# A hybrid decoder block on one Trainium2 core: the projections of attention heads 0 to 3 in three panels of 512 features instead of six of 256

## The chip, the core and the metric

The kernel runs on one core of a Trainium2 chip. The metric is the device time of one execution in microseconds (us). Before the change the median of 3 runs was 982.01 us (981.92 to 983.61). TensorE is called PE here, VectorE DVE, ScalarE ACT, GpSimd POOL; SP is the engine whose queue issues most of the loads.

## What is computed

The block takes x (512 tokens by 1024 features, float32), normalises it to u, and projects u by one combined weight. Branch A is a gated delta rule (GDN) over chunks of 64 tokens, branch B is causal softmax attention with a forgetting bias (FOX), both of 8 heads of 128. The two are merged by gates, and an MLP follows. Cut from the reference:

```python
u = rmsnorm(x, norm_mix_g[l])
proj = u @ w_in[l]
(gq, gk, gv, gz, ga, gb, fq, fk, fv, ff, gate_a, gate_b) = jnp.split(proj, split_idx, axis=-1)
...
o_a = gated_delta_rule_chunked(qh, kh, vh, g, beta).transpose(0, 2, 1, 3)
...
fqh = rmsnorm(to_heads(fq, FOX_HEADS), fox_q_norm_g[l]).astype(f32)
fkh = rmsnorm(to_heads(fk, FOX_HEADS), fox_k_norm_g[l]).astype(f32)
fvh = to_heads(fv, FOX_HEADS).astype(f32)
log_f = jax.nn.log_sigmoid(ff.astype(f32) + fox_f_bias[l].astype(f32)).transpose(0, 2, 1)
o_b = forgetting_attention(fqh, fkh, fvh, log_f).transpose(0, 2, 1, 3)
...
merged = jax.nn.sigmoid(gate_a) * y_a + jax.nn.sigmoid(gate_b) * y_b
h = x + merged @ w_out[l]

hn = rmsnorm(h, norm_mlp_g[l])
x = h + jnp.square(jax.nn.relu(hn @ w_up[l])) @ w_down[l]
```

The change concerns `fq`, `fk` and `fv` of FOX heads 0 to 3: 4 heads x 3 x 128 = 1536 of the projected features, each a sum over 1024.

## The kernel before

**Split products.** A float32 operand is held as two parts, `hi` (rounded to the type that PE multiplies fast) and `lo` (the rest). Each product is made as hi·hi, hi·lo and lo·hi into the same PSUM bank.

**Units of weights.** Weights come in units of 128 x 1024 elements (512 KB). `load` (L200) puts a unit into one of three `raw` buffers by a DMA on SP's queue; `prefetch_split` (L243) casts it to `hi` on ACT (L256) and subtracts to `lo` on DVE (L257), into a pool `whl` that has four hi's and four lo's; `unit` (L260) hands out the next unit and keeps the splits two units ahead and the loads three ahead. A `raw` buffer is free once its `lo` is made, and a `hi` or `lo` once its last product is.

**PSUM.** `mmps` (L92) deals out three banks of 128 x 512 for the projections, in turn. Before a bank is filled again, what was in it must have been copied out.

**The stages** in the order of the program: the start and the first z gates (to 42 us); GDN group 0 (four heads); `fox_pair(0)` and `fox_pair(1)` (L950, about 122 to 213 us); three more z gates and GDN group 1 (to 325 us); a stream of projections for FOX heads 4 to 7 and the gates (L1011, to 535 us); the merge (to 620 us); the MLP (L1171, to 980 us).

**fox_pair** makes, for two heads, three panels of 256 features: q and k of the one head, q and k of the other, v of both. A panel takes two units, `us`, each with four of the eight slices of u's features. For each pair of token blocks (`t2`) one bank is taken; its left half is the first token block and its right half the second. Each token block gets 8 products hi·uhi (L961), 8 of hi·ulo (L962) and 8 of lo·uhi (L964), each 128 x 128 times 128 x 256. Then the bank is copied to the page `fqk`, whole on ACT (L969) for q and k, or half on ACT and half on DVE (L972) for v.

**Beside it** run generators: `tick()` (L127), which fox_pair calls after each token block's first block and after each bank (24 times in the two calls), lets each go on to its next `yield`. Those that matter here are, in this stretch,

- `head` and `invert` (L659) of GDN group 0: `kk` (L639) gives AT (L641), ACT lays out `dg` (L666), DVE transposes it to E (L669) and makes 31 x 2 steps of forward substitution in X (L681, L683), then Xd (L689) and XT (L692). ACT copies Xd into X2 (L698, L699) and XT into AT (L712). PE makes Qp (L707) from Xd, Tp and Tq (L720, L722) from a copy of it (L710), and then Q6 (L741) and T6 (L739);
- `fox_worker` (L866): the head's fq and fk are normalised (fss, L884 and L885), transposed (L898, L899), and its scores, softmax, and output follow (L919 to L947);
- `factors_u` (L426): loads four pages `ux` from DRAM (L432, SP's queue), scales them (L436, ACT), adds and subtracts (L448, DVE) and splits them (L286, L287). It is started between the two calls of fox_pair.

A list scheduler then orders each engine's instructions, ahead of time; on the chip every engine works its list in that order, and an instruction that waits holds up all behind it.

## Time and profile before

| what | value |
| --- | --- |
| median of 3 runs | 982.01 us (981.92 to 983.61) |
| span of the profiled execution, first to last instruction | 980.2 us |
| PE busy | 970.8 us, 99% |
| DVE, ACT, POOL busy | 710.9 (73%), 605.0 (62%), 240.2 us (25%) |
| granted PE clock | full in every slice of the span |
| DMA | 174.38 MB, mean 178 GB/s |

The profiled execution's own time is its span and what lies around it; only the span is shown. In the profile a line such as "124.44 0.96 PE fx L964 x8" in the chain is a start, a length and a count of instructions, and "fqk<-fx 128x512" in the timeline is an output, an input and the shape of one instruction; what stands in brackets is the time that the engine stood idle before, and whose end it had waited for. "L961 PE MATMUL ... x192 | 48.5, 288" is a group, its busy time in us and the mean ns of one; for PE these overlap, so that the steps from start to start are read from the chain.

### The profile page before, as it was taken

What the parts mean: (1) busy time and instruction counts of PE and PEld (TensorE: products, weight loads), DVE (VectorE), ACT (ScalarE), POOL (GpSimd) and SP (SyncE); (2) the same over time, 40 slices, a digit from 0 to 9 for tenths busy, and PEclk for the clock granted to TensorE, in tenths of its full rate; (3) what the DMA queues carried; (4) which work ended last, traced back from release to release, by engine and by line L of the source; (5) the groups of instructions that cost most, each with busy time, mean ns of one, the idle gap of its engine ahead of it and who ended that gap; (6) DMA issues with size and microseconds to landing.
All of it is one profiled execution on the core that took longest, in us unless ns stands there. A gap on an engine that the chain in (4) does not pass through costs nothing.

```text
span 980.2 us, 17198 instructions
## 1 busy us (share of the span) xinstructions
PE 970.8 (99%) x6545; PEld 874.8 (89%) x6545; DVE 710.9 (73%) x1204; ACT 605.0 (62%) x1050; POOL 240.2 (25%) x236
## 2 busy tenths in 40 slices
PE   8999999999999999999999999999999999999998
PEld 6788899998888999999999888889989989988986
DVE  6877778566577789855656535889896697698596
ACT  7766444766564787867656422678755765666761
POOL 1544120202533513522320005312121121121110
PEclk9999999999999999999999999999999999999999
DMA  7647662475437885757887735688798888889884
GB/s 266 213 135 223 174 158 90 130 239 181 129 116 228 189 166 141 197 129 166 236 201 215 273 103 171 125 181 173 190 188 196 187 173 206 181 175 202 186 166 119
DMA packets 93442, 174.38 MB, mean 178 GB/s; under 512 B 8016, under 2 KB 49200, under 8 KB 93360
## 3 DMA queue, kind: packets, MB, share of 16 engines
q1 hardware_dynamic: 78928, 120.85, 38.8%
q0 software_dynamic: 14432, 52.44, 30.5%
q8 instruction: 51, 0.84, 0.4%
q14 instruction: 31, 0.25, 0.1%
HBM read 152.25 MB, written 21.02 MB: 177 GB/s over the span
## 4 chain that ended last, share of the span: by engine, by line
PE 92%; DVE 4%; DMA 2%; ACT 1%; issue 1%; SPq 0%; DVEq 0%
PE mlp L1171 36%; PE st L1011 12%; PE mm L279 8%; PE mm L276 8%; PE mm L275 8%; PE fx L964 2%; PE fx L961 2%; PE fx L962 2%; PE fo L944 2%; PE sc L919 1%; PE pT L935 1%; DVE lo L257 1%; PE kk L639 1%; PE kq L647 1%; DMA ux<-ud 1%; PE v L797 1%
## 5 line engine op out<-in xcount | busy, mean ns | idle before, releaser
L1402 ACT CAST hi<-draw 128x1024 fp32r<-128x1024 f32 x124 | 130.0, 1050 | 118.4 <-PE mlp L1171 100.4
L1409 DVE TENSOR_TENSOR lo<-draw,hi 128x1024 fp32r<-128x1024 f32 x124 | 151.3, 1222 | 44.8 <-ACT hi L1402 41.6
L256 ACT CAST hi<-raw 128x1024 fp32r<-128x1024 f32 (+1 forms) x62 | 62.9, 1021 | 82.6 <-PE mm L276 59.5
L1171 PE MATMUL mlp<-hi,shi 128*128 128x512 f32 x280 | 109.5, 391 | 0.1
L1171 PE MATMUL mlp<-hi,slo 128*128 128x512 f32 x280 | 109.1, 390 | 0.0
L1171 PE MATMUL mlp<-lo,shi 128*128 128x512 f32 x280 | 109.0, 389 | 0.0
L257 DVE TENSOR_TENSOR lo<-raw,hi 128x1024 fp32r<-128x1024 f32 (+1 forms) x62 | 73.9, 1197 | 29.1 <-ACT hi L256 13.4
L1171 PE MATMUL mlp<-shi,lo 128*128 128x256 f32 x448 | 90.3, 283 | 0.0
L1171 PE MATMUL mlp<-slo,hi 128*128 128x256 f32 x448 | 90.3, 283 | 0.0
L1171 PE MATMUL mlp<-shi,hi 128*128 128x256 f32 x448 | 90.3, 283 | 0.0
L276 PE MATMUL mm<-ulo,hi 128*128 128x512 f32 x216 | 85.0, 394 | 1.2 <-DVE ulo L290 1.2
L275 PE MATMUL mm<-uhi,hi 128*128 128x512 f32 x216 | 85.0, 395 | 0.0
L257 DVE TENSOR_TENSOR lo<-sraw,hi 128x1024 fp32r<-128x1024 f32 x49 | 60.7, 1240 | 20.9 <-ACT hi L256 20.1
L1171 PEld LDWEIGHTS mlp<-shi,hi 128*128 128x128 f32 x448 | 70.6, 192 | 0.9
L1171 PEld LDWEIGHTS mlp<-shi,lo 128*128 128x128 f32 x448 | 69.9, 192 | 0.0
L1171 PEld LDWEIGHTS mlp<-slo,hi 128*128 128x128 f32 x448 | 69.8, 192 | 0.0
L256 ACT CAST hi<-sraw 128x1024 fp32r<-128x1024 f32 x49 | 51.3, 1047 | 26.6 <-PE st L1011 16.2
L1171 PEld LDWEIGHTS mlp<-hi,shi 128*128 128x128 f32 x280 | 52.6, 188 | 11.1 <-issue 0.7
L1171 PEld LDWEIGHTS mlp<-lo,shi 128*128 128x128 f32 x280 | 52.6, 188 | 11.1
L1171 PEld LDWEIGHTS mlp<-hi,slo 128*128 128x128 f32 x280 | 52.6, 188 | 10.3
L219 POOL DMA_DIRECT2D draw<-w_d x30 | 26.3, 876 | 129.9 <-DVE lo L1409 120.8
L219 POOL DMA_DIRECT2D draw<-w_u x32 | 27.7, 866 | 122.6 <-DVE lo L1409 120.0
(336 smaller groups left out, 2466.6 us busy)
## 6 DMA issues: line engine op xcount, KB each, us to landing
draw<-w_u POOLq DMA_DIRECT2D x32, 512.0 KB, 5.7
draw<-w_d POOLq DMA_DIRECT2D x32, 512.0 KB, 6.5
sraw<-w_st POOLq DMA_DIRECT2D x28, 512.0 KB, 5.9
draw<-w_d SPq DMA_DIRECT2D x26, 512.0 KB, 4.4
raw<-w_gdn SPq DMA_DIRECT2D x24, 512.0 KB, 3.8
draw<-w_u SPq DMA_DIRECT2D x24, 512.0 KB, 4.4
sraw<-w_st SPq DMA_DIRECT2D x21, 512.0 KB, 5.5
hd<-hd SPq DMA_DIRECT2D x34, 256.0 KB, 5.4
```

What stands on the lines that cost most here:

```text
L219: nc.gpsimd.dma_start(raw, a[w][c, q, s_], accum_op=ALU.add)
L256: act.copy(hi[:, c], raw[:, c])
L257: vec.tensor_tensor(lo[:, c], raw[:, c], hi[:, c].bitcast(F32), op=ALU.subtract)
L275: mm(o, w, rhi(k), start=(k == 0), stop=False)
L276: mm(o, w, rlo(k), start=False, stop=False)
L279: mm(o, lo[:, k * cols:(k + 1) * cols], rhi(k), start=False, stop=(k == KT - 1))
L944: mm(po[:, cs(i)], vt[c], st[i][:, cs(c)], start=(c == 0), stop=(c == i))
L961: mm(o, uhi[k][:, cs(tb)], w, start=(k == 0), stop=False)
L1011: mm(o, u, w, start=first and t == 0 and k == 0 and j == 0 and x is hi, stop=x is lo and k == 3, skip_group_check=True)
L1171: return (lambda *args, **kw: tc.keep_in_program_order(f(*args, **kw))) if self.pinned[0] else f
L1402: pact.copy(hi, raws[m][0])
L1409: pvec.tensor_tensor(lo, raws[m][0], hi[:, :].bitcast(F32), op=ALU.subtract)
```

## The change

fox_pair, called twice with three panels of 256 features, becomes `fox_panel`, called three times with a panel of 512 features: q and k of heads 0 and 1, v of heads 0 to 3, q and k of heads 2 and 3. A panel takes four units, each with two of the eight slices of u's features. It makes two passes (`half`) over them; in a pass two banks are open, each for one token block and all 512 features, and a unit's products go to both. In the first pass the units are taken one after the other, and they are held for the second: `held` stops prefetch_split at the panel's four units, and in the second pass it is raised by one after each unit, with the split and the load called from there. After each unit comes a `tick()`: 8 in a panel, 24 in all. A bank is copied out on ACT alone, as two copies of 128 x 256 (one for each head) or one of 128 x 512 (v). v of all four heads is there after the second panel; factors_u starts after the first. The weights' layout in DRAM follows the panels.

```diff
+    held = [None]
+
     def prefetch_split(n):
-        while len(units) < min(len(seq), n):
+        while len(units) < min(len(seq), n, len(seq) if held[0] is None else held[0]):
...
-    def fox_pair(hp):
-        vts = ([], [])
-        for pn in range(3):
-            us = [unit("w_fox"), unit("w_fox")]
-            pg2 = [page(s="fqk"), page(s="fqk")]
-            for t2 in range(2):
-                ps = mmps("fx")
-                for tb in (2 * t2, 2 * t2 + 1):
-                    o = ps[:, (tb % 2) * 256:(tb % 2 + 1) * 256]
...
+    def fox_panel(heads):
+
+        n0 = pos[0]
+        held[0] = n0 + 4
+        us = []
+        pgs = {h: [page(s="fqk"), page(s="fqk")] for h in heads}
+        vp = []
+        for half in range(2):
+            ps = {tb: mmps("fx") for tb in (2 * half, 2 * half + 1)}
+            for j in range(4):
+                if not half:
+                    us.append(unit("w_fox"))
+                hi, lo = us[j]
+                for tb, o in ps.items():
+                    for k in (2 * j, 2 * j + 1):
+                        w = hi[:, (k % 2) * T:(k % 2 + 1) * T]
                         mm(o, uhi[k][:, cs(tb)], w, start=(k == 0), stop=False)
                         mm(o, ulo[k][:, cs(tb)], w, start=False, stop=False)
+                for tb, o in ps.items():
+                    for k in (2 * j, 2 * j + 1):
+                        mm(o, uhi[k][:, cs(tb)], lo[:, (k % 2) * T:(k % 2 + 1) * T], start=False, stop=(k == KT - 1))
+                if half:
+                    held[0] = n0 + 5 + j if j < 3 else None
+                    prefetch_split(n0 + 5 + j)
+                    prefetch_raw(n0 + 6 + j)
+                tick()
+            for tb, o in ps.items():
+                if heads:
+                    for i, h in enumerate(heads):
+                        act.copy(pgs[h][half][:, (tb % 2) * 256:(tb % 2 + 1) * 256], o[:, i * 256:(i + 1) * 256])
                 else:
+                    v = page(s="fqk")
+                    act.copy(v, o)
+                    vp.append(v)
+        for h in range(G):
+            vts[h].extend(v[:, cs(h)] for v in vp)
+        for h in heads:
+            fq.append((h, pgs[h], vts[h]))
...
-    fox_pair(0)
+    fox_panel((0, 1))
     fu = start(factors_u())
-    fox_pair(1)
+    fox_panel(())
+    fox_panel((2, 3))
```

Lines of the changed kernel are 2 later than before from L245 on, and 12 later behind fox_panel (L970 and L971 are the products with hi, L974 those with lo, L983 and L986 the copies). The order of each engine is the same in both kernels up to the first panel, and nearly so from the stream of projections on. Three places between show what moves. A name such as `fx_262` is a bank's content, and the number tells one from the next.

PE, before, around the start of the sixth panel's first bank (`fx_359`): the products of `fx_325` end, those of the next bank begin, and Qp comes 19 products later.

```order
L964 MATMUL fx_325_2017<-lo_269_1656,uhi_20_185 128x256
L964 MATMUL fx_325_2017<-lo_269_1656,uhi_21_186 128x256
L961 MATMUL fx_359_2168<-hi_296_1827,uhi_14_179 128x256
L962 MATMUL fx_359_2168<-hi_296_1827,ulo_22_187 128x256
...
L964 MATMUL fx_359_2168<-lo_297_1828,uhi_16_181 128x256
L707 MATMUL Qp_310_1875<-Xd_293_1819,AT_87_588 32x32
```

PE, in the change, in the second half of the V panel: the last products of `fx_262` and `fx_263` (the first half's banks), then the 24 products of `fx_307`, then Qp, and behind Qp the other bank of this half, `fx_308`.

```order
L974 MATMUL fx_262_1538<-lo_254_1506,uhi_21_186 128x512
L974 MATMUL fx_263_1539<-lo_254_1506,uhi_20_185 128x512
L974 MATMUL fx_263_1539<-lo_254_1506,uhi_21_186 128x512
L970 MATMUL fx_307_1711<-hi_234_1414,uhi_14_179 128x512
...
L974 MATMUL fx_307_1711<-lo_254_1506,uhi_21_186 128x512
L709 MATMUL Qp_312_1730<-Xd_300_1693,AT_87_588 32x32
...
L709 MATMUL Qp_313_1731<-Xd_300_1693,AT_87_588 32x32
L970 MATMUL fx_308_1712<-hi_234_1414,uhi_14_179 128x512
```

Qp now stands between the two banks of one half. With three banks, `fx_307` has the one that was free, and `fx_308` has that of `fx_262`.

ACT, before, around the copies of the inversion of group 0 (X2 from Xd, AT from XT, Q from Qp): the copy of the bank `fx_304` stands behind them, and behind a softmax step (p, bias).

```order
L698 COPY X2_295_1823<-Xd_293_1819 32x16x32
L699 COPY X2_295_1823<-Xd_293_1819 32x16x32
L712 COPY AT_87_588<-XT_294_1821 32x16x32 x4
L710 COPY Q_309_1874<-Qp_310_1875 32x512
...
L969 COPY fqk_302_1839<-fx_304_1841 128x512
L436 ACTIVATE ux_312_1915<-ux_312_1915,c_norm_mix_g_118 128x512
```

ACT, in the change, at the same copies and on to the next bank's copies.

```order
L700 COPY X2_302_1697<-Xd_300_1693 32x16x32
L701 COPY X2_302_1697<-Xd_300_1693 32x16x32
L714 COPY AT_87_588<-XT_301_1695 32x16x32 x4
L288 CAST hi_303_1703<-ux_297_1677 128x512
L986 COPY fqk_305_1707<-fx_262_1538 128x512
L986 COPY fqk_306_1709<-fx_263_1539 128x512
L712 COPY Q_311_1729<-Qp_312_1730 32x512
...
L438 ACTIVATE ux_333_1893<-ux_333_1893,c_norm_mix_g_118 128x512
L745 ACTIVATE AT_87_588<-T6_340_1919 64x8x64
L986 COPY fqk_343_1940<-fx_307_1711 128x512
L986 COPY fqk_344_1942<-fx_308_1712 128x512
```

The copies of `fx_262` and `fx_263` stand behind X2, AT and a cast of factors_u, and those of `fx_307` and `fx_308` behind factors_u's next `ux`; the first group of `ux` is scaled ahead of X2.

SP, before: the last units of w_fox, three of w_z, and then the loads of `ux`.

```order
L227 DMA raw_353_2158<-w_fox 128x1024
L227 DMA raw_356_2164<-w_z 128x1024
L227 DMA raw_395_2385<-w_z 128x1024
L227 DMA raw_398_2391<-w_z 128x1024
L432 DMA ux_312_1915<-ud_347 128x512
```

SP, in the change: the first group of `ux` stands ahead of the last two units of w_fox, and the second group (`ux_333`) behind three of w_z.

```order
L434 DMA ux_277_1590<-ud_347 128x512
L227 DMA raw_299_1679<-w_fox 128x1024
L757 DMA hd_326_1870<-hd0_589 128x512
L227 DMA raw_325_1868<-w_fox 128x1024
L757 DMA hd_327_1872<-hd0_589 128x512
L757 DMA hd_328_1874<-hd0_589 128x512
L227 DMA raw_339_1917<-w_z 128x1024
L227 DMA raw_370_2030<-w_z 128x1024
L227 DMA raw_388_2090<-w_z 128x1024
L434 DMA ux_333_1893<-ud_347 128x512
```

Where one group of `ux` was loaded in this stretch there are now two, and the second one follows the w_z loads as the first did in before.

## The prediction

> **What bounds the kernel now.** I read the page first, then the table by stage, then TensorE's waits, then the chain.

> ```profile
> span 980.2 us, 17198 instructions
> PE 970.8 (99%) x6545; PEld 874.8 (89%) x6545; DVE 710.9 (73%) x1204; ACT 605.0 (62%) x1050; POOL 240.2 (25%) x236
> PEclk9999999999999999999999999999999999999999
> 122.00:213.50 91.50, 91.02 (x928) 89.05 (x927) 60.10 (x147) 52.20 (x104) 14.35 (x14) 1.00 0.50 151
> PE Q L741 <- ACT AT L725: 0.5, 1, 0.5
> ```

> The first three lines are the page: PE is busy 99% of the span at a full granted clock. The fourth is the stretch of the two calls of fox_pair: PE is busy 91.02 of 91.50 us. The last is the whole answer on what PE waits for between 115 and 330 us: one wait of 0.5 us. So PE is the bound there; a product saved ends the kernel earlier by its own time, and a new wait of PE ends it later by its own length. The profiled span is 980.2 us and the median 982.0, so 1.8 us lie around the span; I take them as unchanged, and add any difference to 982.0. About 2 us (0.2%) is what a measurement of this kernel can tell from no change.

> **The change: the products.** These rows give a product's step, from the chain (start, length, count), and the counts by line.

> ```profile
> 106.58 1.81 PE mm L279 x8
> 120.70 1.83 PE mm L279 x8
> 124.44 0.96 PE fx L964 x8
> 506.98 20.15 PE st L1011 x168
> L961 PE MATMUL fx<-hi,uhi 128*128 128x256 f32 x192 | 48.5, 288 | 0.0
> ```

> A product over 256 columns takes 0.96/8 = 0.120 us, and 20.15/168 = 0.120 over a long run; one over 512 takes 1.81/8 = 0.226 to 1.83/8 = 0.229; I take 0.227. L961 has 192 products, and so have L962 and L964, which stand in the same loops: 576 x 0.120 = 69.1 us. The change does the same work in 288 products over 512: 288 x 0.227 = 65.4. It saves 3.7 us (3.2 at 0.229), and all of it lies on the path.

> [...]

> **What moves.** In before a PSUM bank takes two token blocks, and a bank that is closed isn't needed again until two more have been filled: 96 products, 11.5 us. In the change two of the three banks are open at once, and in the V panel's second half the order of PE runs one block's 24 products after the other's. The bank of a half's second block is the one that the half before filled first. Between its close and its new start stand the 24 products of one block: 24 x 0.227 = 5.4 us, and what lies between. So the copies that empty a bank have half the time. How late do they come now?

> ```profile
> 166.02 0.96 PE fx L964 x8
> 171.78 0.96 PE fx L964 x8
> 172.78 0.61 ACT L698 COPY X<-Xd 32x512 f32<-32x512 f32 x1
> 173.40 0.62 ACT L699 COPY X<-Xd 32x512 f32<-32x512 f32 x1
> 174.24 2.50 ACT L712 COPY AT<-XT 32x512 f32<-32x512 f32 x4 [0.22 <-DVE XT L692]
> 178.97 0.56 ACT L969 COPY fqk<-fx 128x512 f32<-128x512 f32 x1
> 186.91 0.57 ACT L969 COPY fqk<-fx 128x512 f32<-128x512 f32 x1
> ```

> The first two are the last products of two banks: they are closed at 167.0 and 172.7. Their copies start at 178.97 and 186.91, 12 and 14 us later, since ScalarE works in a fixed order in which the inversion of head group 0 (X from Xd, AT from XT) stands ahead of them. In before that cost PE nothing. In the change it does, and the order says where: ScalarE's copy of the V panel's first bank stands behind the same X2 and AT copies, and PE's second block waits for it.

> **When X is ready.** Everything there hangs on VectorE's inversion, whose rows in before are these.

> ```profile
> 135.33 0.89 PE kk L639 x8
> 137.22 1.12 DVE L641 SCALAR_TENSOR_TENSOR AT<-kk,ssk,eb 128x128 f32<-128x128 f32 x4
> 138.38 2.51 ACT L666 COPY dg<-AT 32x512 f32<-32x512 f32 x4 [0.96 <-DVE AT L641]
> 141.07 2.08 DVE L669 STREAM_TRANSPOSE E<-dg 128x1024 f32<-128x1024 f32 x1
> 138.26 0.67 DVE L884 TENSOR_REDUCE fss<-junk 128x4 f32<-128x512 f32 x1
> L681 DVE TENSOR_TENSOR tmp<-E,X 128x126 f32<-128x126 f32 (+22 forms) x31 | 8.6, 278 | 0.9
> L683 DVE TENSOR_TENSOR X<-X,tmp 128x126 f32<-128x126 f32 (+22 forms) x31 | 7.9, 256 | 1.0
> L257 DVE TENSOR_TENSOR lo<-raw,hi 128x1024 fp32r<-128x1024 f32 x4 | 4.9, 1223 | 1.6 <-PE fx L964 1.6
> 170.48 1.19 DVE L689 STREAM_TRANSPOSE Xd<-X 128x512 f32<-128x512 f32 x1
> 173.50 0.70 DVE L692 STREAM_TRANSPOSE XT<-Xd 128x512 f32<-128x512 f32 x1
> 125.40 0.44 PE ktm L119 x4
> 175.02 1.13 PE Qp L707 x64
> ```

> In before Xd ends at 171.67 and PE comes to Qp, which reads it, at 175.02: 3.3 us to spare. In the change I count both forward from the same place. PE, from the panels' start at 122.5: 96 products of panel 1 (21.8), three transposes as ktm's (1.3), kk and kq (1.8): 147.4. The first half of panel 2, 48 x 0.227: 158.3. Its second half's first block, 5.4, and eight transposes of head 0 as ktm's (0.9) with a switch or two: Qp at **164.8**. VectorE: kk stands behind 48 products (10.9) and the three transposes and ends at 135.6 (136.2 in before). AT 1.1, dg 2.5 and E 2.1, with a small gap after kk: 141.7. The chain of 62 steps (L681, L683) is 16.5 busy with 1.9 idle ahead of its steps; inside it stand, as in before, four lo's (4.9) and the fss step (0.7, and 0.2 for a small one behind it); the copies of L972 are gone. Then 1.2 of Xd: 167.1. Without the idle it would be 165.2, with another microsecond of waits for lo's 168.1; I take **167.1**. PE has gained on VectorE and waits 2.3 us at Qp.

> **First wait, the V panel's second half.** After Qp (1.2) PE would begin the second block at 166.1 without any wait. ScalarE has, after Xd: X2 twice (1.23), AT four times (2.50, XT is there in time), and a cast of half a page (about 0.6, as X2's copies of 512 columns), then the copy of the bank (0.58) and a gap or two: 5.2 in all, so 172.3. The bank had been ready since 158.3. Loss against 166.1: **6.2 us**, of which 2.3 are the wait at Qp; 4.0 if Xd comes at 165.2 and nothing lies between ScalarE's steps (4.9), 7.2 if it comes at 168.1.

> **Second wait, panel 3.** Its second block waits for the copy of the V panel's third bank. ScalarE has this copy behind the first `ux` scaling of factors_u, which the change starts one panel earlier; its load stands on SP's queue behind three loads of w_z, and the last of these waits until a raw buffer has been split.

> ```profile
> 163.20 12.47 SPq L227 DMA_DIRECT2D raw<-w_z  x3
> ux<-ud SPq DMA_DIRECT2D x4, 256.0 KB, 5.5
> 181.02 2.06 ACT L436 ACTIVATE ux<-ux,c_norm_mix_g 128x512 f32<-128x512 f32 x3 [1.49 <-DMA ux<-ud]
> 177.15 7.02 DMA ux<-ud
> raw<-w_fox SPq DMA_DIRECT2D x12, 512.0 KB, 4.7
> row<-rowd SPq DMA_DIRECT2D x24, 256.0 KB, 6.9
> 185.54 1.11 PE Q L741 x16
> ```

> In before SP held these three w_z loads for 12.47 us, and ux landed 5.5 us after its issue (median of four), with ScalarE idle for it. In the change: PE runs 24 products from 172.3 with Tp and Tq (1.8) among them, to 179.6. The fourth unit's buffer is read until 179.1; its hi (1.05, behind Tp's two copies) ends at 180.9, its lo (1.2) at 182.2. SP then issues w_z and ux at 182.8, ux lands at 188.5 to 189, is scaled (0.72), one copy of AT (0.5) and the bank's copy follow: 191.0. PE comes there after 24 products (5.4), Q6 and T6 (0.5, 1.1 and 0.5), scores and a wait of 0.8 for Q6s: 188.2. Loss: **2.8 us**, between 0 (a load as fast as w_fox's 4.7 takes 0.8 off; an earlier lo the rest) and 4.3 (7.0, as ux's last one).

> **The small ones.** The wait for Q6s, 0.8, takes the place of before's 0.5 (that wait goes). Panel 3's last block waits for copies behind p's transposes and a weight's cast: about 1.1, the length of one cast that is ahead; between 0 and 2. Less copying on VectorE (the four L972 copies go) and more on ScalarE (16 of 128x256 where there were 8 of 128x512 and four) changes nothing but this order. The weights are the same 12 units; that a panel holds its four units lets new ones be split only as the second half frees them, and the order puts their casts ahead of PE's need: PE's first product of panel 3 comes at 179.6, its hi is cast after 173. That cover is 3 to 5 us; were it gone, up to one cast and one lo (2.3 us) would be added.

> **Sum.** -3.7 + 6.2 + 2.8 + 0.8 + 1.1 - 0.5 = +6.7 us; 982.0 + 6.7 = **988.7**. With the low ends, -3.7 + 4.0 + 0 + 0.5 + 0 - 0.5 = +0.3: 982.3. With the high ends, the saving at 0.229 (3.1), -3.1 + 7.2 + 4.3 + 0.8 + 2 + 2.3 - 0.5 = +13.0: 995.0.

> **Rivals.** (1) *The waits don't form, the products decide: faster.* For it: every bank that is copied late in before was harmless, and the saving is certain. It needs the copy done 6.2 us earlier than I count: a place ahead of X2, or Xd that much earlier. -3.7, and -0.5 where the old wait goes too: 978 us. Against it: VectorE has only 0.8 us of copies to lose. It decides where the copies end before 166.1, and before PE's second block of panel 3. 0.14. (2) *The low end*: the first wait at 4.0 and none of the others, +0.3: 982.3, inside 980 to 984. 0.10. (3) *Loads that stack up: slower still.* The `row<-rowd` loads, as large as ux's, take 6.9 us in the median; were ux in the change to wait out half or all of one such load, with the w_z loads and the hd loads ahead of it, it would come 3.4 to 6.9 us later than 188.5, of which PE pays all: 992.1 to 995.6. 0.12. (4) *A clock that falls.* PE would stand still 3.9 us (6.2 less 2.3) before the second block. No row of this trace shows what comes after such a pause, for PE has none. If its products ran at half speed for as long again as the pause, 3.9 us of time would do half its work: +2, and 990.7. 0.10. [...]

> **How the numbers follow.** My own sum has 0.54, rival (1) 0.14, (2) 0.10, (3) 0.12, (4) 0.10. The range must leave out no more than 0.2: from 980.5, above rival (1), to 995.0, the sum's high end, with 0.06 beyond it (the worst of rivals 3 and 4). The likeliest case alone has 982.3 to 995.0. Faster by over 0.2% (below 980.0): 0.14. Within it: (2), 0.10. Slower: 0.76.

> **What would show it.** Right: the fx products as 288 steps of 0.227; a wait of PE at Qp for Xd (2 us) and, right behind Qp, one for ScalarE's copy of the V panel's bank (about 4 us; 4.0 to 7.2 for both), with ScalarE's copies X2 and AT just ahead; then one for a copy behind ux, with SP's w_z before it; the span from 325 us on shifted, not changed. Wrong: PE busy throughout with the V copy done ahead of X2 (rival 1); a step of 0.23 where 0.12 was saved twice, by which there would be no saving; a granted clock under 1.00 in the slice around 170 us (rival 4); or PE waiting for hi's or lo's of w_fox, which I say are covered.

## The result, and the profile after

Before and after were run on one chip, four times each: 982.2 us (981.92 to 983.61) and **994.6 us** (994.2 to 996.73). The ratio is 1.0126, with a 95% interval of 1.011 to 1.0142: the change costs 12.4 us. The profiled execution has a span of 992.7 us against 980.2, 12.5 more. The page of the changed kernel, its totals and the granted clock in 40 slices:

```profile
span 992.7 us, 16622 instructions
PE 972.5 (98%) x6257; PEld 862.3 (87%) x6257; DVE 710.5 (72%) x1200; ACT 605.1 (61%) x1056; POOL 240.5 (24%) x236
PEclk9999999899999999999999999999999999999999
```

PE runs 288 instructions fewer, and its busy time has not fallen (972.5 against 970.8). The eighth slice of the clock, 174 to 199 us, shows an 8: a mean over 24.8 us, which does not give the place. Where the time went is told by the starts of two lines, in before and in the change: the first product of the panels, and the first of the stream that follows GDN group 1 (times at the end of a row: first and last start). First before:

```profile
L961 PE MATMUL fx<-hi,uhi x192: 278/283/368, 122.4 to 212.1; 128*128 128x256 f32 x192
L1011 PE MATMUL st<-hi,hi x224: 277/283/681, 331.3 to 533.8; 128*128 128x256 f32 x112
```

And the change:

```profile
L970 PE MATMUL fx<-hi,uhi x96: 387/389/796, 122.1 to 220.2; 128*128 128x512 f32 x96
L1023 PE MATMUL st<-hi,hi x224: 277/283/681, 342.9 to 545.5; 128*128 128x256 f32 x112
```

The panels begin at the same time and the stream 11.6 us later; only 0.9 us are added behind it. So nearly the whole loss lies between 122 and 343 us. PE's waits there, in the change (us in total, times, the longest; `mm` is a bank of the other projections, `conv` a page of the convolution ahead of GDN's q, k and v, `pT` transposed softmax weights of FOX):

```profile
PE Qp L709 <- DVE Xd L691: 4.7, 1, 4.7
PE fx L970 <- ACT fqk L986: 3.2, 1, 3.2
PE mm L277 <- DVE conv L601: 2.2, 1, 2.2
PE fx L970 <- ACT fqk L983: 0.4, 1, 0.4
PE T L741 <- DVE Q6s L748: 0.4, 1, 0.4
PE mm L277 <- ACT proj L1094: 0.3, 1, 0.3
PE pT L937 <- DVE sso L770: 0.2, 1, 0.2
```

These are 11.4 us where before had 0.5. The first two are those that the prediction named. The chain through them (start, length), with two products of 512 columns from 20 us later at the end:

```profile
168.11 1.07 DVE Xd L691
169.20 0.62 ACT X L700
...
170.46 0.62 ACT AT L714
...
172.34 0.61 ACT AT L714
172.98 0.62 ACT hi L288
173.59 0.50 ACT fqk L986
174.13 0.80 PE fx L970
174.93 0.43 PE fx L971
...
199.34 0.45 PE fx L974 x2
```

ScalarE does X twice, AT four times, a cast, and only then empties the V panel's bank, as the order had it. Behind the two pauses a product takes 0.43 us, where two take 0.45 later on. A table by stage, cut at the places where the granted clock changes (stretch, length, PE busy and count, ..., PEclk, DMA share, GB/s), shows why:

```profile
166.16:169.58 3.42, 0.36 (x22) 0.36 (x24) 3.08 (x11) 0.38 (x1) 0.51 (x1) 1.00 0.00 0
169.58:172.99 3.41, 1.34 (x54) 1.20 (x46) 0.97 (x3) 3.33 (x7) 0.00 (x0) 0.50 0.01 2
172.99:176.41 3.42, 2.28 (x5) 1.82 (x6) 2.15 (x4) 2.69 (x6) 0.00 (x0) 0.50 0.00 0
176.41:179.82 3.41, 3.41 (x9) 2.64 (x8) 3.23 (x6) 2.66 (x4) 0.00 (x0) 0.50 0.02 5
179.82:183.23 3.41, 3.41 (x106) 2.71 (x105) 3.23 (x5) 1.54 (x3) 0.00 (x0) 1.00 0.81 273
```

The clock is at half from 169.58 to 179.82 us. PE is busy for 1.34 + 2.28 + 3.41 = 7.0 us of it and does half the work: 3.5 us lost.

**The account** up to the stream's start (from 122.4 to 331.3 in before, 208.9 us; from 122.1 to 342.9 in the change, 220.8: +11.9): the waits +10.9 (11.4 less 0.5), the half clock +3.5, the products -3.7, together +10.7. The rest, 1.2 us, can lie in what the view of waits does not show. It counts idle time from the modelled end of a product, 0.39 us after its start for 512 columns, while the next could start after 0.227; by this estimate a wait behind such a product costs about 0.16 us more than it shows, and seven make 1.1 at most. With the 4.6 us that e6 below shows for the products, in place of 3.7, some 0.9 us more stay unexplained.

### The profile page after: what moved, and what is told of

The parts are those of the page before. It is cut to its first block, busy times and chain, and to the rows that moved or that the text cites. A ratio compares the mean times of both kernels' runs of the same rounds, so it can differ in the third digit from the quotient of the medians.

```text
span 992.7 us, 16622 instructions
## 1 busy us (share of the span) xinstructions
PE 972.5 (98%) x6257; PEld 862.3 (87%) x6257; DVE 710.5 (72%) x1200; ACT 605.1 (61%) x1056; POOL 240.5 (24%) x236
## 4 chain that ended last, share of the span: by engine, by line
PE 86%; DVE 7%; ACT 3%; DMA 3%; issue 1%; SPq 0%; DVEq 0%; ACTq 0%
PE mlp L1184 35%; PE st L1023 11%; PE mm L281 8%; PE mm L277 8%; PE mm L278 8%; PE fo L946 2%; PE fx L970 2%; DMA row<-oad 1%; PE fx L971 1%; PE sc L921 1%; PE fx L974 1%; DVE tmp L683 1%; DVE lo L259 1%; DVE X L685 1%; PE pT L937 1%
## 5 line engine op out<-in xcount | busy, mean ns | idle before, releaser
L258 ACT CAST hi<-sraw 128x1024 fp32r<-128x1024 f32 x49 | 51.3, 1047 | 28.7 <-PE st L1023 14.4
## 6 DMA issues: line engine op xcount, KB each, us to landing
draw<-w_u POOLq DMA_DIRECT2D x32, 512.0 KB, 5.8
draw<-w_d POOLq DMA_DIRECT2D x32, 512.0 KB, 6.5
sraw<-w_st POOLq DMA_DIRECT2D x28, 512.0 KB, 6.4
draw<-w_d SPq DMA_DIRECT2D x26, 512.0 KB, 4.6
raw<-w_gdn SPq DMA_DIRECT2D x24, 512.0 KB, 4.1
draw<-w_u SPq DMA_DIRECT2D x24, 512.0 KB, 4.5
sraw<-w_st SPq DMA_DIRECT2D x21, 512.0 KB, 5.0
hd<-hd SPq DMA_DIRECT2D x34, 256.0 KB, 4.9
```

The costliest lines, as they stand in the source:

```text
L258: act.copy(hi[:, c], raw[:, c])
```

## The experiments

Four theories were held against each other. **A**: X comes late, and ScalarE's order puts the bank's copies behind X2 and AT; put the copies ahead and the loss goes. **B**: three banks and four split units are too few for two open banks and four held units. **C** (formed after the first four runs): PE waits at the inversion's serial steps (Qp, Tp, Q6, T6) wherever the order leaves too little product work between them, and runs at half clock afterwards; the copies are only one place for it. **D**: the loss belongs to open banks and held units, wherever the inversion lies. Beside these stands the earlier start of `factors_u`, the change's other part. Each ratio below is to runs of the kernel before made beside the experiment, whose medians were 981.88 to 982.22 us; e2, e3, e4, e7, e8 and e9 have two runs each.

### e1: the copies ahead of the inversion

```diff
-                tick()
+                if j < 3:
+                    tick()
             for tb, o in ps.items():
...
+            tick()
```

The tick of a half's last unit comes after the copies.

> Theory A (the late X): the change's loss is PE's wait at Qp for Xd (4.7 us), its wait for the V panel's bank, whose copy stands behind X2 and AT on ScalarE (3.2), and the half clock after both (2.7). Here a half's banks are copied out before the last tick of that half, so the copies stand ahead of X2, and Qp moves behind more products: all three go, 994.6 - 10.6 = 984.0, or 981 to 982 if the wait of 2.2 us in GDN group 1 goes as well. Theory B (three banks of 512 columns and four held units are too few, wherever the copies stand): PE waits for the next bank or unit instead, and the time stays at 990 or more.

994.94 us (994.46 to 995.86), ratio 1.0132 (1.0116 to 1.0149): no gain. Both waits are gone, and others stand in their place. PE's waits, and two stretches by stage:

```profile
PE T L741 <- DVE Q6s L748: 2.7, 1, 2.7
PE D L576 <- POOL gu L575: 2.1, 3, 1.4
PE Tp L722 <- ACT Q L712: 1.7, 1, 1.7
...
```

```profile
178.58:181.99 3.41, 2.33 (x101) 2.25 (x102) 2.83 (x6) 1.68 (x4) 0.00 (x0) 1.00 0.91 286
181.99:185.40 3.41, 1.42 (x15) 1.23 (x12) 2.63 (x7) 1.01 (x3) 0.00 (x0) 0.50 0.64 246
```

The copies now stand ahead of ScalarE's part of the inversion, so PE reaches its next step, Tp, before Q is there, then Q6 and T6 the same way; and the clock halves here too, for 10.2 us (182.0 to 192.2), and for 6.8 us more from 274 on. A as I had it falls: the loss isn't tied to the place of the copies. This is where C comes from.

### e2: a fourth bank

```diff
-NMM = 3
+NMM = 4
```

> Four banks for the projections instead of three, and four for the rest instead of five; the copies stay behind X2 and AT. Theory A: Qp stands behind both of the half's banks, so PE doesn't wait for Xd; the first bank of panel 3 needs the copy that ends at about 174 and PE comes there at about 171: one wait of 2 to 3 us, too short for the clock to fall: 986 to 988. Theory B, in its form of too few banks: about 984 or less, since the bank is then no bound at all; in its form of too few units: as the change, 994.

1014.37 us (1013.22 to 1015.52), ratio 1.0329 (1.0307 to 1.0351). The fourth bank is taken from the five that serve everything else. Qp still waits (3.8 us), though A had said that it would not, and so does fx (3.4). In the whole run PE waits 7.2 us for conv (2.2 in the change), 4.5 at the stream's first products and 2.6 at pT, and the panels begin 8 us later (130.5 against 122.1), so that the smaller pool, or the other order, costs much elsewhere. That a wait of 2 to 3 us is too short for the clock to fall was an estimate, and it came both ways: the clock stayed at 1.00 beside 2.2 us at conv in the change and 2.5 in e10, and fell to 0.50 behind 2.2 in e5 and 2.1 in e6. Against B only as far as it goes: PE waited for Xd with the bank there.

### e3: half of the substitution

```diff
         for j in range(B - 1):
+            if rest == INV_STEP[0] and j % 2:
+                continue
```

> Leaves out every second one of the 31 pairs of forward substitution of GDN group 0 (30 of 62 steps of VectorE, about 8 us; the solution of group 0 is then another one), everything else as in the change. Theory A: Xd comes 8 us earlier, the copies behind it too, so both waits and the half clock go: about 984. Theory B: no difference beyond the wait at Qp: 989 to 990.

1003.95 us (1003.03 to 1004.87), ratio 1.0223 (1.0202 to 1.0244): slower with less work. Xd is early, and there is no wait at Qp; but the inversion's generator reaches its later steps sooner, everything behind them moves, and PE waits 8.0 us for conv, 3.8 at pT and 1.7 at Tp, with half a clock twice between 171 and 203 us and twice more, 3.4 us each, from 287.6 and 308.1 on. Leaving steps out moved the order more than the time of X; as a test of A it decides nothing, and it fits C.

### e4: factors_u one panel later

```diff
-    fu = start(factors_u())
     fox_panel(())
+    fu = start(factors_u())
```

> factors_u starts after the second panel instead of after the first. On ScalarE the V panel's copies then stand right behind X2 and ahead of AT, and no ux load stands on SP's queue ahead of the weights. Theory A: the wait at Qp stays (3 to 5 us), the wait behind it falls from 3.2 to under 1; with a pause of 4 us or more the clock still falls: 989 to 992; if the pause is under about 3.5 us and the clock stays up, 987. If factors_u were the cause of it all (a third theory): 982 or less.

995.15 us (994.17 to 996.14), ratio 1.0133 (1.0112 to 1.0154). The wait behind the copies is gone, the one at Qp is the same 4.7 us, and 1.7 us each have come at conv and at omT (a transpose in GDN group 1). By stage:

```profile
165.17:168.59 3.42, 0.00 (x0) 0.00 (x0) 2.94 (x15) 0.00 (x0) 0.25 (x1) 1.00 0.00 0
168.59:172.00 3.41, 2.36 (x65) 2.27 (x66) 2.08 (x3) 2.35 (x5) 0.27 (x1) 0.50 0.00 0
172.00:175.41 3.41, 3.41 (x9) 2.64 (x9) 0.32 (x1) 3.33 (x6) 0.00 (x0) 0.50 0.00 0
```

One pause of 4.7 us is followed by 6.8 us at half clock here; another 3.4 us follow a pause in GDN group 1, at 274.4. The 3.5 and 4 us of the expectation were estimates: the clock fell behind 4.7 us here, and behind 2.2 in e5. The waits came as theory A had put them, the time did not (989 to 992).

### e5: PE kept busy through both waits

```diff
+        if rest == INV_STEP[0]:
+            for i in range(20):
+                mm(pqs[0][:, :], uhi[0][:, 0:P], uhi[1], start=True, stop=True)
...
+        tpb = [atps("Tp") for _ in range(2)]
+        if rest == INV_STEP[0]:
+            for i in range(14):
+                mm(tpb[0][:, :], uhi[0][:, 0:P], uhi[1], start=True, stop=True)
```

Products that nobody reads, into banks that are written anew afterwards, fill the two pauses: 20 x 0.227 = 4.5 us ahead of Qp and 14 x 0.227 = 3.2 behind it. Nothing comes earlier by it; only the clock can change.

> The change, with 34 further products of 128x512 that nobody reads: 20 ahead of Qp and 14 behind it, written into the banks of Qp and Tp before those are filled, so that PE works where it waited 4.7 and 3.2 us. Theory C (the clock falls because PE stands nearly still there, and the half clock costs by itself): the waits stay as long, filled with work, but the 13 products behind them take 0.23 instead of 0.43 us: 991 to 992. If the clock fell for another reason, or cost nothing: 994.6 or more, by up to 1 us for products that don't fit.

992.03 us (991.54 to 992.19), ratio 1.01 (1.0085 to 1.0116), 2.6 us less than the change. By stage:

```profile
170.00:175.00 5.00, 4.67 (x55) 3.62 (x48) 1.88 (x5) 4.90 (x9) 0.00 (x0) 1.00 0.02 5
```

PE is busy for 4.67 us of this stretch, and the clock stays whole, where it had been 0.50. In return the 2.2 us pause at conv is followed by half a clock here, which it was not in the change (3.4 us, so 1.7 lost). The last product of the panels starts at 220.7 instead of 223.4, 2.7 us earlier. That is about half of PE's busy time behind the second pause, (2.28 + 3.41) / 2 = 2.8; the slow Qp, 0.7, had been hidden in the wait for the copy behind it. The stream starts 1.0 us earlier (341.9 instead of 342.9), which is 2.7 less the 1.7; why 2.6 are measured in all is not shown. So the fall of the clock behind the two pauses is a cost of its own beside the waits, 2.7 us.

### e6: copies first, factors_u later, and the inversion in smaller steps

```diff
-INV_STEP = (2500, 900)
+INV_STEP = (1300, 900)
```

with the edits of e1 and e4. `INV_STEP` is the work after which the inversion's generator yields; a smaller one spreads its steps over more ticks, and so over more products.

> The change with three places moved: a half's banks copied out before its last tick (as in the first experiment), factors_u after the second panel (as in the fourth), and a yield after about half as many steps of the forward substitution of group 0 (1300 instead of 2500), so that Qp, Tp, Q6 and T6 stand 2 to 3 blocks of products later on PE. Theory C (the loss is PE's waits at the inversion's serial steps and the half clock behind them, wherever the order puts too few products between those steps): nearly all of 12.5 us goes and the 3.7 us of the products are seen: 979 to 981. Theory D (two open banks of three, and four held units, cost it whatever the order): 988 or more.

984.85 us (983.69 to 985.95, eight runs), ratio 1.003 (1.002 to 1.004), span 983.6: 9.7 us better than the change, and still slower than before. All of PE's waits between 115 and 345 us:

```profile
PE mm L277 <- DVE conv L601: 3.9, 3, 2.1
PE D L576 <- POOL gu L575: 0.4, 1, 0.4
PE o L820 <- ACT vn L801: 0.2, 1, 0.2
```

None of these lies in the panels: in this order two open banks and four held units cost PE no wait there, which speaks against B and against D (988 or more). C's 979 to 981 was missed as well. The panels' products, counted from the starts of the trace, each to the start of what follows, make 67.3 us in place of 71.9: the work saved is there. The waits that are left lie in GDN group 1, where before had none. The chain of the longest:

```profile
293.35 2.22 POOL conv L654
295.59 0.36 SPq L543
296.00 6.06 DMA hd<-conv
302.17 0.70 ACT conv L598
...
306.16 0.75 DVE conv L601
307.04 0.47 PE mm L277
```

GpSimd finishes a conv page, SP stores it (6.06 us), and ACT, which is to fill the page anew, waits until the store has landed; VectorE and PE stand behind ACT.

### e7: the smaller steps alone

The change with `INV_STEP` at 1300, and nothing else.

> The change with the yields alone (1300 instead of 2500). Theory C: no wait at Qp for Xd, as Qp stands three blocks later; the copies stand behind the first ux instead, so a wait of 2 to 3 us may stay at a bank: 984 to 988. Theory D: 992 or more.

996.07 us (996.06 to 996.07), ratio 1.0143 (1.0124 to 1.0161): pT waits 2.5 us, Qp 2.1, conv 2.2, and the clock is at half for 10.2 us from 179 on, 6.8 from 206 and 3.4 from 318.5. By the figures put down ahead this is D's (992 or more): C had said that Qp would not wait. Yet e6, with the same panels, stands against D. Each of e6's three edits alone is worth nothing; together they are worth 9.7 us.

### e8: before, with factors_u one panel earlier

```diff
         for pn in range(3):
+            if hp == 0 and pn == 2:
+                fu.append(start(factors_u()))
```

in the kernel before, which keeps its panels of 256.

> The kernel before, with one part of the change alone: factors_u starts one panel earlier (after 8 of the 24 ticks, as in the change). If this start is what throws the order out (third theory), 986 or more; by theories C and D it is the panels: 981 to 984.

991.02 us (990.2 to 991.85), ratio 1.0092 (1.0073 to 1.011): 9.1 us slower, without any of the change's panels. PE's waits, 115 to 345 us:

```profile
PE mm L275 <- DVE conv L599: 3.2, 1, 3.2
PE sc L919 <- issue: 1.7, 1, 1.7
...
```

The longest is again the one in GDN group 1, with 3.4 us at half clock behind it (272.7 to 276.1). These waits, 4.9 more than before's, and the 1.7 of the clock make 6.6 of the 9.1; the rest is not explained. The figure is that of the third theory (986 or more), and C and D, which had 981 to 984, missed it. The panels are thus not the only way to lose that time: an earlier generator is another. With e4, where the later start gained nothing, it also says that the two parts' costs don't add.

### e9: one bank at a time

```diff
-        for half in range(2):
-            ps = {tb: mmps("fx") for tb in (2 * half, 2 * half + 1)}
+        for tb in range(4):
+            half = tb // 2
+            ps = {tb: mmps("fx")}
```

Four passes with one bank, as few open banks as before, the units held for all four. The ticks move too: they stand behind the second unit and, as in e1, behind a bank's copies.

> The change with one part undone: one bank open at a time, so four passes over the panel's four held units, with 24 products of a token block after one another and two other banks to cover its copies; 24 ticks as in the change, panels of 512. Theory C (the order of the inversion's serial steps): the same waits at Qp or at Tp and T6, 992 to 996. Theory D in its form of too few banks: the loss goes, 980 or less; in its form of held units: slower than the change, 997 or more.

998.16 us (996.38 to 999.94), ratio 1.0164 (1.0144 to 1.0183). PE waits 3.8 us at Tp for ACT's Q, 2.3 at pT, 1.1 for a hi of a weight, and runs at half clock for 10.2 us from 183 on and twice for 3.4 us in GDN group 1. So the loss stays with one open bank: two are not needed for it, and the waits stand where e1 has them. The time lies above C's figure and in that for held units (997 or more), but the two runs lie on both sides of it; this run does not clear the held units.

### e10, e11, e12: attempts at a version that gains

e10 is e6 with half of the copies on VectorE and a page's store held back by one tick in place of two:

```diff
-LATE = 2
+LATE = 1
...
+                        (vec.tensor_copy if i else act.copy)(pgs[h][half][:, (tb % 2) * 256:(tb % 2 + 1) * 256], o[:, i * 256:(i + 1) * 256])
...
+                    (vec.tensor_copy if tb % 2 else act.copy)(v, o)
```

> The sixth kernel, with half of the panels' copies on VectorE and the delay of late stores one tick shorter (LATE 1 for 2), so that the buffers that GDN group 1's conv waits for are stored sooner. By theory C the panels' stretch stays without waits and the waits of 2.1 and 1.5 us in GDN group 1 shrink: 979 to 982. If that stretch loses the same with any other order: 984 to 985.

985.6 us (983.48 to 987.0, six runs), ratio 1.0035 (1.0022 to 1.0049): no better than e6. The panels have no wait, and conv has 4.3 us in three. e11 is e6 with one page more, so that a page is needed again less soon after its store:

```diff
-NPG = 53
+NPG = 54
```

> The sixth kernel with one thing changed, 54 pages instead of 53. There PE's last wait in GDN group 1 (2.1 us, with half a clock behind it) came from a conv page that was still being stored to DRAM (hd from conv, 6.4 us) when its turn came again; with 54 pages the pages fall to other tiles and that conv waits for a page freed earlier. If the page is the cause, that wait goes and 2 to 4 us with it: 981 to 983. If the stretch would only wait for something else: 984 to 986.

984.11 us (983.37 to 986.6, twelve runs), ratio 1.0018 (1.0007 to 1.003). conv's longest wait goes from 2.1 to 1.5 us, and the clock stays whole in the profile. Over all runs its mean was 0.997 or 0.998 in 3 of 12, against 4 of 8 in e6, and the intervals of the two ratios overlap: what the page is worth is not clear of the noise. e12 is e10 with the page:

> The tenth kernel with 54 pages instead of 53: the wait of 2.5 us there hung on the same page. If the page is the cause: 981 to 983; else 984 to 986.

983.45 us (982.64 to 985.72, twelve runs), ratio 1.001 (1.0002 to 1.0019): the best version with the wide panels, and not faster than before. The longest of PE's waits between 115 and 345 us; the others are 0.3 and 0.2:

```profile
PE mm L277 <- DVE conv L601: 3.2, 3, 1.5
```

All together that is 3.2 us more than before, which eats most of the 3.7 that the products save. By these two e12 would be 0.5 us faster; it is 1.3 slower, and where the difference lies is not shown.

## Why the prediction was right, and where its terms were not

The direction held, and so did the mechanism of the first wait, which is the largest part: 982.2 + 12.4, in the range and near its upper end, where 6.7 was forecast. That the range held it is luck in part. Its upper end was reached with 4.3 us of a second wait and 4.3 of small ones, of which 0.4 came; the half clock (3.5) and GDN group 1 (2.5), which the sum left out, came in their place. By the steps:

- **The products.** Right. Two take 0.45 to 0.46 us, 0.227 each. From start to next start the panels' products fall from 71.9 us to 67.3 in e6, where no wait is among them: 4.6, of which 3.7 are the steps and the rest the switches between.
- **When PE is at Qp.** Right: 164.8 forecast; it is 169.22 less a wait of 4.72, 164.5.
- **When X is ready.** Off: 167.1 forecast, 169.2 measured. The cause is seen in VectorE's timeline (start, length, instruction, idle before):

```profile
149.39 1.23 DVE L259 TENSOR_TENSOR lo<-raw,hi 128x1024 fp32r<-128x1024 f32 x1 [2.23 <-ACT hi L258]
...
154.35 0.29 DVE L685 TENSOR_TENSOR X<-X,tmp 128x126 f32<-128x126 f32 x1
154.68 1.12 DVE L683 TENSOR_TENSOR tmp<-E,X 128x120 f32<-128x120 f32 x1
155.84 1.00 DVE L685 TENSOR_TENSOR X<-X,tmp 128x120 f32<-128x120 f32 x1
```

  A lo of w_fox stands in the middle of the substitution and waits 2.23 us, as its hi waited 3.60 for the load. I had called the weights covered, by 3 to 5 us. They were, for PE; not for X, which sits behind them on VectorE. SP's issues of w_fox show why the load was late:

```profile
142.56 3.77 SPq L227 DMA_DIRECT2D raw<-w_fox  x3
```

  These are the first since 123.58, where before has issues at 123.88 and 136.20. They wait for a raw buffer, which the lo at 141.34 frees, the first one since 122.32: `held` keeps the next panel's units from being split until the second pass. The same gap stands in e6 (123.96 to 142.93) and in e9 (125.41 to 147.33), which hold units as well. So the held units seem to reach X by way of VectorE; this was read from the rows and not tested by itself. Two steps of the substitution also took 1.12 and 1.00 us in place of 0.29, 1.5 more, beside GpSimd's work:

```profile
154.62 2.08 POOL L891 TENSOR_TENSOR fqk<-fqk,fss 128x512 f32<-128x512 f32 x2
```

  One step had been slow in before as well (0.91 us for 0.21, at 143.49), so the 62 steps took 17.5 us where the 16.5 of before were taken over. The 1.9 us of idle in the sum are the small gaps ahead of the steps, which are here too (2.0); for a wait ahead of a lo it had nothing, though before's row of L257 shows 1.6. So the error of 2.1 us is in the main the lo's wait, then the slower steps, less small gains (E ended 0.3 us earlier).
- **The first wait.** Right in its place and in its two parts, wrong in size: 4.7 + 3.2 = 7.9 for 6.2, above the 7.2 that I gave as its high end. The bank's copy ends 4.9 us after Xd (174.09 less 169.17), for which I had 5.2; the error is X's.
- **The clock.** This is the step that failed most. I held it as a rival to my own sum, with 0.10, though nothing in it excludes the sum: once PE waits, both come together, and the sign that I had listed against my sum, a clock under 1.00 around 170 us, came together with the two waits that I had listed for it. It belonged into the sum as a term. Its price was 2: half speed for as long again as a pause of 3.9 us, an assumption that no row of before shows. The runs show a clock of 0.50, for 10.2 us in the change and for 6.8 in e4. In the account that is 3.5 us, of which 2.7 went into the time (e5).
- **The second wait**, 2.8, did not form. The copy behind ux ended at 193.5, 2.5 later than forecast, since ux was scaled at 191.26; but PE came at 194.3 and not at 188.2. PE had moved by 6.1 us and the copy by 2.5, so what PE lost earlier was taken off this wait.
- **The small ones.** Q6s took 0.4 for 0.8, the copies behind p 0.4 for 1.1. No wait of PE there ends with a hi or lo of w_fox; what the held units cost goes by way of X. Rival (3), loads that stack up, gives 992.1 to 995.6 and so this time, but by another way: no wait of PE ends with a load of ux.
- **GDN group 1.** Not in the prediction: "shifted, not changed" held from the stream on, but I said it from 325 us on and priced nothing between the panels and there. That stretch lost 2.2 + 0.3 us.

So the theory after the runs is C, and it has a second place. By it PE is busy 99% of the time in before since at each serial step of the inversion, and at each conv of group 1, the order has enough products between. Wider panels, other copies, an earlier generator or fewer steps each rearrange both places. C tells in each trace where time went; it did not forecast the time of a new order. Its figures for e6 to e10 were all too low, by 2 to 8 us; that for e5 came.

What has been shown is that the clock takes a share of its own (e5), that neither the copies' place (e1) nor the later generator (e4) nor the smaller steps (e7) takes the loss away alone, that the loss stays with one open bank (e9), that an earlier generator costs time without the panels (e8), and that wide panels can run without a wait among them (e6, e10 to e12). What stays open is how the change's loss divides between the panels and the earlier generator, how much of X's delay belongs to the held units, and why no order of group 1 tried here is as good as before's: the page that is still being stored explains at most 0.6 us of the longest wait (e11).

## What to carry to other kernels

Where one engine is busy 99% of the time, ask what each change of order takes away as cover from the serial steps of the others, ahead of counting the instructions it saves: here 3.7 us of work were saved and 14.4 (10.9 + 3.5) lost to waits and clock. Work that hides one engine's load may stand in front of another engine's chain, so cover has to be asked for each engine apart. A pause of PE of some microseconds is priced with the half clock behind it, as a term and not as a rival: here 10.2 us at 0.50 came with pauses of 4.7 and 3.2 us, and cost 3.5 beside them.

## What was not expected of the hardware

```profile
292.46:295.87 3.41, 2.51 (x15) 1.84 (x13) 3.41 (x9) 1.56 (x2) 0.00 (x0) 1.00 0.34 91
295.87:299.29 3.42, 2.12 (x9) 1.80 (x10) 3.42 (x8) 2.18 (x3) 0.00 (x0) 1.00 0.84 165
```

In e5 the same pause lies in one window, PE is busy for 1.25 us of it, and the next is at half:

```profile
292.32:295.73 3.41, 1.25 (x6) 1.06 (x7) 3.41 (x9) 1.99 (x3) 0.00 (x0) 1.00 0.90 70
295.73:299.14 3.41, 3.41 (x10) 2.63 (x9) 3.34 (x6) 1.13 (x2) 1.67 (x2) 0.50 0.55 149
```

The same follows 1.28 us in e6 (304.90 to 308.31). In e1 it fell behind 2.33 us (178.58 to 181.99), while in the change it stayed behind 2.12, in the second row above. So how long PE is busy in a window does not settle it alone; what else does is not shown. In the change, in e1 and at 168.59 in e4 the clock came back behind a window in which PE was busy throughout, 3.41 us at half clock, but later in e4 this one was enough:

```profile
274.40:277.81 3.41, 2.93 (x7) 2.38 (x8) 3.41 (x6) 2.27 (x3) 3.35 (x4) 0.50 0.27 77
```

Less did not bring it back: 2.28 us in the change (172.99 to 176.41), 2.36 in e4 (168.59 to 172.00) and 2.69 in e1 (185.40 to 188.82). Of the eight runs of e6, the four with a mean clock of 0.998 took 985.3 to 986.0 us, and the four with 0.999 or 1.000 took 983.7 to 984.4.

**VectorE beside GpSimd.** In the change two steps of 120 elements a row took 1.12 and 1.00 us, where the step of 126 ahead of them took 0.29, beside a product of two operands on GpSimd. GpSimd's two instructions, of 1.04 and 1.08 us, end at 155.66 and 156.70, and the two slow steps 0.14 us behind them, at 155.80 and 156.84. In before the slow step, of 0.91 us, ended at 144.40, 0.05 us behind a product on GpSimd (144.35). What holds the steps up is not shown.
